# The second frame block turned once and copied out, its steps placed between the passes of the first products

## The chip, the cores and the metric

The kernel runs on one core of one Trainium2 chip. The core has five engines that run side by side: TensorE (PE, matrix products and transposes), VectorE (DVE), ScalarE (ACT), GpSimd (POOL) and SyncE (SP, which here only issues transfers). The metric is the device time of one execution in microseconds (us), as the median of the runs shown. Times of single steps come from the trace of one profiled execution.

## The reference, cut to what matters

One layer of a trunk works on 2048 prompt frames and 32 sample frames (2080 rows, 1024 wide). What concerns the change is the normalisation of the frames and the first projection:

```python
def rmsnorm(x, g):
    y = x32 * lax.rsqrt(jnp.mean(x32 * x32, axis=-1, keepdims=True) + EPS)
    return (y * g.astype(jnp.float32)).astype(x.dtype)

def layer(h, p, ...):
    hn = rmsnorm(h, g_mix)
    proj = hn @ w_in
    hA, bA, cA, zA, vB, zB = jnp.split(proj, ...)
    yA, new_conv = short_conv_mixer(hA, bA, cA, zA, ...)
    yB, new_pool = pooling_mixer(vB, zB, ...)
    h = h + jnp.concatenate([yA, yB], axis=-1) @ w_out
    gate = jax.nn.sigmoid(rmsnorm(h, g_ple) @ w_ple_gate)
    h = h + (p @ w_ple) * gate
    return h, new_conv, new_pool
```

`w_in` has 6 times 512 columns (h, b, c, za, v, zb). A final normalisation closes the trunk.

## The kernel before, in words

**Split numbers.** Products run on values split in two parts, a rounded high part and the remainder (hi and lo). One product is three matmuls: hi times hi, hi times lo, lo times hi. ScalarE makes the hi part by a copy with a cast (line 77), VectorE the lo part by a subtraction (line 78); `put` and `split` do both.

**Blocks, groups, units.** The 2080 frames are five blocks of 416 (`NB`); groups 0 and 1 have two blocks each, group 2 the last. The projection is done in units: one group and one of four 128-wide column slices `j`. Unit 0 is plain (`Unit.plain`): for each of six weights (zb, v, c, then h, za, b) and each of the two blocks, eight chunks of the 1024 rows times three split terms are 24 matmuls of 128x416 (line 571; the very first one, zb of block 0, by line 586 in the order of its split terms). Units 1 to 7 use seven half products in place of eight (`Unit.seven`, `pair`) on sums of the frames (`B["T1"]` to `B["T4"]`) and sums of the weights (`pair_weights`). Units 1 to 3 store two of these weight sums in memory (`kept_...`, lines 552 and 553), and units 4 to 7 load them again.

**Frames.** A block is three tiles of 128 frames and a short one of 32; the short tile of block 1 shares its load with that of block 0 (`short0`). A tile is loaded (line 392), its sum of squares is taken on ScalarE (line 88), the reciprocal root on GpSimd (lines 69 and 73), VectorE scales it by this and the gain row `g_bc` (`normal`, line 406), TensorE turns it in two halves of four 128x128 transposes into a bank of PSUM (`turn`, line 413), and the bank is split into the frames' pieces `B`. The gain row itself is spread over the partitions by two matmuls (`gm`, line 375) and copied by VectorE (line 376).

**Second block.** `second_block` is a generator. Its steps are: three loads with sums and normals; four turnings of which the pieces "12" and "22" are split (`pt1`); and four steps that turn the tile once more (`pt2`) and make from the two banks and the first block's pieces the sums T1 to T4 (line 619, with a ScalarE copy of one bank in line 626). `Unit.plain` calls a step between its products by hand: two behind zb, two behind v and three behind c of block 0, then one each at later places.

**Later columns.** While units 1 to 3 run, `next_columns` prepares the second group's frames column by column (the short column first, then 0, 1, 2): loads, sums, normals, turnings (`pt_g`, kept in program order), and seven pieces that are staged in tiles and stored by GpSimd's queue (line 482). The staged tiles and the frame tiles share one ring of five places (`xin`). The frames of the following column are loaded at step 5 of a column.

**Order.** Each engine runs its instructions in one order; a scheduler fills it in from dependences, and `keep_in_program_order` (or the flag `later`) holds single instructions at the place where the code has them. Transfers are issued in order by the queue of an engine: SP's for loads and stores of results, GpSimd's for the staged and the kept stores. PSUM has eight banks: six of the ring `bank` and two of the ring `tbank`.

Of the kernel before, what the change touches and what calls it, by code (L numbers as in the profile page):

```python
# [9 lines left out]
F32 = mybir.dt.float32  # L10
# [24 lines left out]
def trunk(ctx, tc, x_p, x_s, c_conv, c_pool, p_p, p_s, g_mix, w_in, conv_w, conv_b, pool_w,  # L35
# [19 lines left out]
    def tbank(name):  # L55
        return ps_t.tile([P, 512], F32, tag="tr", name=name)
# [273 lines left out]
    with ExitStack() as s1:  # L330
# [38 lines left out]
        nc.sync.dma_start(gm_row, g_mix)  # L369
        ones = ftile("ones").rearrange("p k n -> p (k n)")[:1, :P]  # L370
        nc.vector.memset(ones, 1.0)
        for half in range(2):
            cs = slice(half * NH, half * NH + NH)
            pg = tbank(f"gm_{half}")
            nc.tensor.matmul(pg, ones, gm_row[:, cs], start=True, stop=True)
            nc.vector.tensor_copy(g_bc[:, cs], pg)


        hn = {}
# [21 lines left out]
        def x_tile(name, rows):  # L401
            return x_stat(x_load(name, rows))
# [123 lines left out]
        def pair_weights(gi, ka, kb, j, name, ring, s_ring):  # L526

            s_t = (wk.tile([P, KH, P], F32, tag="s", bufs=1, name=f"s_{name}") if s_ring is None else
                   s_ring(f"s_{name}"))
            ra = raw_weight(ka, j, f"{name}a", ring)
            a11, a12 = ra[:, :KH], ra[:, KH:]
            sub = lambda o, x, y: nc.vector.tensor_tensor(o, x, y, op=ALU.subtract)
            if (ka, j) in kept:
                k1, k3 = kept.pop((ka, j))
                rb = ring(f"raw_{name}b")
                col = cols[kb] * WA + j * P
                nc.sync.dma_start(s_t, k1)  # L540
                nc.sync.dma_start(rb[:, :KH], k3)
                nc.sync.dma_start(rb[:, KH:], w_in[NH:, col:col + P].rearrange("(k p) n -> p k n", p=P))
                s3, a22 = rb[:, :KH], rb[:, KH:]
            else:
                rb = raw_weight(kb, j, f"{name}b", ring)
                a21, a22 = rb[:, :KH], rb[:, KH:]
                nc.vector.tensor_tensor(s_t, a21, a22, op=ALU.add)
                sub(a21, a11, a21)
                s3 = a21
                if gi == 0:  # L550
                    kept[ka, j] = k1, k3 = [tc.dram_tile([P, KH, P], F32, name=f"kept_{name}_{q}") for q in (1, 3)]
                    nc.gpsimd.dma_start(k1, s_t)
                    nc.gpsimd.dma_start(k3, s3)
            src = {"11": a11, "12": a12, "S2": a11, "S1": s_t, "S3": s3, "S4": a12, "22": a22}

            def make(q):
                if q == "S2":
                    sub(a11, s_t, a11)
                if q == "S4":
# [11 lines left out]
                    nc.tensor.matmul(ps[:, :NB], lhs[:, k, x], b[:, k, y], start=start and k + q == 0,  # L571
                                     stop=stop and k == KH - 1 and q == 2, skip_group_check=True)

        begun = []

        def project(ps, w, tb):
            x = hn[tb]
            if begun:
                for half in range(2):
                    half_product(ps, w[half], x[half], half == 0, half == 1)  # L580
                return

            begun.append(tb)
            steps = sorted(((k, a, b) for k in range(KC) for a, b in ((0, 0), (0, 1), (1, 0))), key=lambda t: t[1:])
            for i, (k, a, b) in enumerate(steps):
                nc.tensor.matmul(ps[:, :NB], w[k // KH][:, k % KH, a], x[k // KH][:, k % KH, b], start=i == 0,
                                 stop=i == len(steps) - 1)


        B0 = {}  # L590
        ahead0 = [x_tile(f"0_{c}", [x_rows(0, c)]) for c in range(3)]
        short0 = x_tile("0_3", [x_rows(0, 3), x_rows(1, 3)])
        B0.update(six(0))
        for c, x in enumerate([*ahead0, short0]):
            normal(x)
            n = P if c < 3 else DEC
            for half, q in enumerate(("11", "21")):
                put(B0[q][:, :, :, c * P:c * P + n], turn(x, half, f"pt0_{c}_{half}", bank)[:, :, :n])
        hn[0] = B0["11"], B0["21"]
        first_w.extend([weights(kind, 0, f"first{kind}") for kind in ("zb", "v", "c")])  # L600
        B0["12"] = piece_of(seventh("B0_12"), 0)
        hn[1] = B0["12"], B0["22"]

        def second_block():

            spans = [(c, slice(c * P, min(NB, c * P + P))) for c in range(4)]
            xs = []
            for c in range(3):
                x = x_tile(f"1_{c}", [x_rows(1, c)])
                normal(x)  # L610
                xs.append((x, slice(0, P)))
                yield
            xs.append((short0, slice(DEC, 2 * DEC)))
            for c, cs in spans:
                x = xs[c][0]
                for half, q in enumerate(("12", "22")):
                    put(B0[q][:, :, :, cs], turn(x, half, f"pt1_{c}_{half}", bank)[:, :, xs[c][1]])
                yield
            op = lambda o, a, b, op=ALU.subtract: nc.vector.tensor_tensor(o, a, b, op=op)
            for c, cs in spans:  # L620
                x, ts = xs[c]
                n = ts.stop - ts.start
                t1, t3, t2, t4 = (ftile(f"f{t}_1_{c}")[:, :, :n] for t in range(4))
                part = lambda q, h: B0[q][:, :, h, cs].bitcast(F32)
                p12 = turn(x, 0, f"pt2_{c}_0")[:, :, ts]
                nc.scalar.copy(t3, p12)
# [42 lines left out]
        class Unit:  # L669
# [98 lines left out]
            def plain(self):  # L768
                tbs, j, tag, zs, V, U, c_s = self.tbs, self.j, self.tag, self.zs, self.V, self.U, self.c_s
                blocks = range(len(tbs))  # L770

                def product_of(kind, b, w):
                    ps = bank(f"{kind}{tag}_{tbs[b]}")
                    project(ps, w, tbs[b])
                    return ps[:, :NB]
# [14 lines left out]
                if len(tbs) > 1:  # L790

                    wc = weights("c", j, f"c{tag}")
                    for b in blocks:
                        zb_block(b)
                        if b == 0:
                            for _ in range(2):
                                next(second)
                        v_block(b)
                        if b:
                            self.mix(b - 1)  # L800
                            next(second)
                        else:
                            for _ in range(2):
                                next(second)
                        c_block(b)
                        if b == 0:
                            for _ in range(3):
                                next(second)
# [697 lines left out]
```

## Time and profile before

| what | us |
|---|---|
| median of 3 runs (lowest to highest) | 945.69 (944.71 to 946.76) |
| the profiled execution | 946.5 |
| its span, first to last instruction | 944.7 |
| TensorE busy | 922.9 |
| VectorE, ScalarE, GpSimd busy | 717.3, 481.3, 137.0 |
| unit 0, from its first product to unit 1's first | 16.44 to 80.86 |
| group 0 (units 0 to 3) and unit 4's start | 16.44 to about 250 |

A row of the timeline gives a start, a length, the engine and the line of the kernel, the operation, output and inputs, the shape, the number of instructions that follow each other, and in brackets how long the engine stood idle in front and what released it. Matmuls overlap, so the time per instruction is read from starts, not from single lengths. PE is TensorE's matmul side, SPq and POOLq are the queues that issue transfers.

### The profile page before, as it was taken

How to read it: one execution, taken by the hardware profiler on the slowest of the kernel's cores; microseconds unless marked ns; L12 is line 12 of the kernel's file. 1: busy time of each engine (PE TensorE's matmuls, PEld its weight loads, DVE VectorE, ACT ScalarE, POOL GpSimd, SP SyncE). 2: the span in 40 equal slices, each digit the busy share in tenths (PEclk: the TensorE clock that was granted, in tenths of full speed). 3: DMA queues.
4: the chain of work that ended last, by engine and by line, in shares of the span. 5: the costliest groups of instructions: out<-in, count | busy, mean ns of one | idle time of the engine just before them, and what ended most of it. 6: DMA issues, size and time to landing. Idle time of an engine off the chain costs nothing.

```text
span 944.7 us, 13128 instructions
## 1 busy us (share of the span) xinstructions
PE 922.9 (98%) x4599; PEld 832.6 (88%) x4599; DVE 717.3 (76%) x1212; ACT 481.3 (51%) x890; POOL 137.0 (14%) x262
## 2 busy tenths in 40 slices
PE   7999999898999999999999999999999999999996
PEld 5999999898999999999999987888878868888885
DVE  6797998788676877776777588766554798888995
ACT  5554555463344554443554356434434885556564
POOL 2202333230100120000000011211111000211113
PEclk9999999999999999999999999999999999999999
DMA  8347686686972554618655349875785884566562
GB/s 252 95 125 199 190 262 215 198 247 182 417 253 90 180 185 131 208 57 291 177 175 174 129 145 315 270 199 159 222 255 160 309 277 127 198 232 222 207 206 111
DMA packets 132639, 190.05 MB, mean 201 GB/s; under 512 B 11740, under 2 KB 101084, under 8 KB 131293
## 3 DMA queue, kind: packets, MB, share of 16 engines
q1 hardware_dynamic: 115149, 134.06, 45.4%
q0 software_dynamic: 14688, 49.65, 16.0%
q10 hardware_dynamic: 2736, 5.51, 1.8%
q8 instruction: 36, 0.59, 0.3%
q14 instruction: 30, 0.25, 0.1%
HBM read 129.59 MB, written 59.58 MB: 200 GB/s over the span
## 4 chain that ended last, share of the span: by engine, by line
PE 77%; DVE 2%; ACT 1%; issue 0%; POOL 0%; POOLq 0%; ACTq 0%
PE x_o L167 9%; PE x_g L167 9%; PE x_zab L571 5%; PE e L102 5%; PE z_g L167 5%; PE x_ch L571 5%; PE x_zbv L571 5%; PE z_o L167 4%; PE z_ch L571 3%; PE z_zbv L571 2%; PE z_zab L571 2%; PE y_g L167 2%; PE y_o L167 2%; PE b L571 2%; PE za L571 2%; PE c L571 2%
## 5 line engine op out<-in xcount | busy, mean ns | idle before, releaser
L77 ACT CAST y_S<-y_fS 128x512 fp32r<-128x512 f32 x32 | 19.5, 621 | 43.9 <-PE x_o L167 19.4
L102 PE MATMUL e<-wq,pps 128*128 128x512 f32 (+1 forms) x156 | 38.9, 399 | 0.2 <-ACT pps L77 0.2
L571 PE MATMUL z_ch<-B,w_ch_S 128*128 128x416 f32 x168 | 35.9, 364 | 3.3 <-ACT U L866 3.3
L406 DVE SCALAR_TENSOR_TENSOR xt<-xt,rstd_x,g_bc 128x1024 f32<-128x1024 f32 (+2 forms) x18 | 23.1, 1282 | 19.1 <-POOL rstd_x L73 17.7
L571 PE MATMUL x_zab<-B,w_zab_S 128*128 128x416 f32 x168 | 34.6, 353 | 2.7 <-ACT V L866 2.0
L571 PEld LDWEIGHTS z_ch<-B,w_ch_S 128*128 128x128 f32 x168 | 32.4, 195 | 4.1 <-ACT U L866 3.6
L167 PE MATMUL x_g<-wg_b,g_S 128*128 128x512 f32 x128 | 35.9, 390 | 0.0
L167 PE MATMUL x_o<-wo_b,y_S 128*128 128x512 f32 x128 | 35.8, 391 | 0.0
L571 PEld LDWEIGHTS x_zab<-B,w_zab_S 128*128 128x128 f32 x168 | 31.1, 188 | 4.0 <-ACT V L866 2.6
L571 PE MATMUL z_zab<-B,w_zab_S 128*128 128x416 f32 x168 | 34.1, 351 | 0.5 <-ACT U L866 0.5
L571 PE MATMUL z_zbv<-B,w_zbv_S 128*128 128x416 f32 x168 | 34.2, 352 | 0.0
L571 PE MATMUL x_zbv<-B,w_zbv_S 128*128 128x416 f32 x168 | 34.1, 351 | 0.0
L571 PE MATMUL x_ch<-B,w_ch_S 128*128 128x416 f32 x168 | 34.0, 351 | 0.0
L102 PEld LDWEIGHTS e<-wq,pps 128*128 128x128 f32 (+1 forms) x156 | 27.4, 182 | 6.9 <-ACT pps L77 0.5
L571 PEld LDWEIGHTS z_zab<-B,w_zab_S 128*128 128x128 f32 x168 | 31.3, 188 | 1.1 <-ACT U L866 0.8
L69 POOL TENSOR_SCALAR ms_f<-ssq_f 128x1 f32<-128x1 f32 (+1 forms) x15 | 8.8, 588 | 160.7 <-ACT junk L88 160.7
L571 PEld LDWEIGHTS x_ch<-B,w_ch_S 128*128 128x128 f32 x168 | 31.4, 188 | 0.3
L571 PEld LDWEIGHTS x_zbv<-B,w_zbv_S 128*128 128x128 f32 x168 | 31.3, 188 | 0.3
L571 PEld LDWEIGHTS z_zbv<-B,w_zbv_S 128*128 128x128 f32 x168 | 31.2, 188 | 0.4
L77 ACT CAST y<-y 128x512 fp32r<-128x512 f32 x24 | 14.8, 618 | 28.7 <-PE x_o L167 14.0
L1328 DVE SCALAR_TENSOR_TENSOR h<-h,rstd_f,g_bc 128x1024 f32<-128x1024 f32 (+1 forms) x15 | 19.3, 1284 | 12.7 <-POOL rstd_f L73 12.7
L167 PEld LDWEIGHTS x_o<-wo_b,y_S 128*128 128x128 f32 x128 | 24.0, 188 | 5.1 <-ACT c_o L1132 0.3
(582 smaller groups left out, 2670.8 us busy)
## 6 DMA issues: line engine op xcount, KB each, us to landing
y<-y_d SPq DMA_DIRECT2D x16, 512.0 KB, 7.7
x<-in_x_prompt_dram SPq DMA_DIRECT2D x16, 512.0 KB, 6.7
h_d<-x SPq DMA_DIRECT2D x16, 512.0 KB, 3.4
h<-h_d SPq DMA_DIRECT2D x16, 512.0 KB, 5.1
xt<-in_x_prompt_dram SPq DMA_DIRECT2D x15, 512.0 KB, 12.0
e<-e_d SPq DMA_DIRECT2D x15, 512.0 KB, 5.1
out_dram<-h POOLq DMA_DIRECT2D x14, 512.0 KB, 3.0
p_dT<-T POOLq DMA_DIRECT2D x12, 512.0 KB, 5.3
```

The source lines that it names most:

```text
L69: nc.gpsimd.tensor_scalar(ms[:n], ssq[:n], scalar1=1.0 / D, scalar2=EPS, op0=ALU.mult, op1=ALU.add)
L77: ins = nc.scalar.copy(hi, src)
L102: nc.tensor.matmul(ps[:n], pps[:, a, k, :n], wp[k][b][:, cs], start=k + q == 0, stop=k == 1 and q == 2)
L167: nc.tensor.matmul(ps[:n], lhs[:, k, a, :n], w[b][:, k], start=start and k + q == 0, stop=k == KH - 1 and q == 2, skip_group_check=True)
L406: nc.vector.scalar_tensor_tensor(xt[:n], xt[:n], r[:n], g_bc[:n], op0=ALU.mult, op1=ALU.mult)
L571: nc.tensor.matmul(ps[:, :NB], lhs[:, k, x], b[:, k, y], start=start and k + q == 0, stop=stop and k == KH - 1 and q == 2, skip_group_chec ...
L1328: nc.vector.scalar_tensor_tensor(h[:n], h[:n], rf[:n], g_bc[:n], op0=ALU.mult, op1=ALU.mult)
```

## The change: what it does

- **Beginning.** The two `gm` matmuls stay in their banks `pg`; block 0's normals multiply from there, in halves of 512 (`first_normal`), and ScalarE copies the gain row out later. Seven, two, three and two transposes of the identity into the short tile's bank are put between the turnings of block 0 (`fill`). The hi and lo parts of block 0 and of the first weights are written out in an order by hand (`first_hi`, `first_lo`), one hi part on VectorE.
- **First products.** zb, v and c of block 0 are computed together (`first_products`), each in a bank of its own, in three passes: hi times hi for all three, then weight hi times frame lo, then weight lo times frame hi. Two steps of the second block (loads and normals of its first two tiles) stand before the second pass, the third tile's before the third pass, and one turning stands before each of the three products of the third pass and one behind them. All are held in program order. The lo parts of v's and c's weights are made in the third pass.
- **Second block.** Each of its tiles is turned once. The bank is split into the pieces and also copied by ScalarE into the tile's own place (`turned`); the sums read that copy. The 32 transposes and four copies of the second turning are gone, eight copies are new.
- **Transfers.** The kept stores go from GpSimd's queue to SP's. The next column's frames are loaded at step 7 of a column, not 5.

```diff
+        pg = [tbank(f"gm_{half}") for half in range(2)]
         for half in range(2):
-            cs = slice(half * NH, half * NH + NH)
-            pg = tbank(f"gm_{half}")
-            nc.tensor.matmul(pg, ones, gm_row[:, cs], start=True, stop=True)
-            nc.vector.tensor_copy(g_bc[:, cs], pg)
+            nc.tensor.matmul(pg[half], ones, gm_row[:, half * NH:half * NH + NH], start=True, stop=True)
+
+        def fill(n, t):
+
+            for _ in range(n):
+                tc.keep_in_program_order(nc.tensor.transpose(t[:, :P], ident, ident))
+
+        short_bank = bank("pt0_3")
+        fill(7, short_bank)
...
-                    nc.gpsimd.dma_start(k1, s_t)
-                    nc.gpsimd.dma_start(k3, s3)
+                    nc.sync.dma_start(k1, s_t)
+                    nc.sync.dma_start(k3, s3)
...
+        def first_products(ws):
+            x = hn[0]
+            out = {kind: bank(f"{kind}0_0_0") for kind in ws}
+            for a, b in ((0, 0), (0, 1), (1, 0)):
+                if b:
+                    next(second)
+                    next(second)
+                for kind, w in ws.items():
+                    if a:
+                        if kind == "zb":
+                            next(second)
+                            first_los["v"]()
+                        elif kind == "v":
+                            first_los["c"]()
+                        next(second)
+                    for k in range(KC):
+                        ins = nc.tensor.matmul(out[kind][:, :NB], w[k // KH][:, k % KH, a], x[k // KH][:, k % KH, b],
+                                               start=a + b + k == 0, stop=a == 1 and k == KC - 1, skip_group_check=True)
+                        if a + b + k or kind != "zb":
+                            in_turn(ins)
+            next(second)
+            return out
...
+        def first_normal(x):
+            xt, m, r = x
+            for half in range(2):
+                h = xt[:m, half * NH:half * NH + NH]
+                in_turn(nc.vector.scalar_tensor_tensor(h, h, r[:m], pg[half][:m], op0=ALU.mult, op1=ALU.mult))
...
+        def first_tile(c):
+            first_normal(first_x[c])
+            turned_x[c] = first_turn(c, first_x[c])
+            if c < 3:
+                fill((2, 3, 2)[c], short_bank)
...
+        for half in range(2):
+            nc.scalar.copy(g_bc[:, half * NH:half * NH + NH], pg[half])
...
             for c, cs in spans:
-                x = xs[c][0]
+                x, ts = xs[c]
+
+                turned = x[0].rearrange("p (k t) -> p k t", k=KC)[:, :, :ts.stop - ts.start]
                 for half, q in enumerate(("12", "22")):
-                    put(B0[q][:, :, :, cs], turn(x, half, f"pt1_{c}_{half}", bank)[:, :, xs[c][1]])
+                    pt = turn(x, half, f"pt1_{c}_{half}", bank)[:, :, ts]
+                    put(B0[q][:, :, :, cs], pt)
+                    nc.scalar.copy(turned[:, half * KH:half * KH + KH], pt)
+                whole.append((turned[:, :KH], turned[:, KH:]))
                 yield
...
-                p12 = turn(x, 0, f"pt2_{c}_0")[:, :, ts]
-                nc.scalar.copy(t3, p12)
                 op(t1, p12, part("11", 0))
-                p22 = turn(x, 1, f"pt2_{c}_1")[:, :, ts]
-                op(t3, p22, t3)
+                op(t3, p22, p12)
...
                     wc = weights("c", j, f"c{tag}")
+                    first.update(first_products(dict(zb=wz, v=wv, c=wc)))
                     for b in blocks:
                         zb_block(b)
-                        if b == 0:
-                            for _ in range(2):
-                                next(second)
                         v_block(b)
...
-                    if i == 5 and after is not None:
+                    if i == 7 and after is not None:
                         load_ahead(1, after)
```

More of the change, by code (lines that the diff above doesn't have):

```diff
@@ L572, in half_product @@
                                      stop=stop and k == KH - 1 and q == 2, skip_group_check=True)
-        begun = []
         def project(ps, w, tb):
             x = hn[tb]
[L578 to L587, printed above, removed]
+            for half in range(2):
+                half_product(ps, w[half], x[half], half == 0, half == 1)
@@ L590, in trunk @@
         B0 = {}
-        ahead0 = [x_tile(f"0_{c}", [x_rows(0, c)]) for c in range(3)]
-        short0 = x_tile("0_3", [x_rows(0, 3), x_rows(1, 3)])
+        ahead0 = [x_load(f"0_{c}", [x_rows(0, c)]) for c in range(3)]
+        short0 = x_load("0_3", [x_rows(0, 3), x_rows(1, 3)])
         B0.update(six(0))
-        for c, x in enumerate([*ahead0, short0]):
-            normal(x)
-            n = P if c < 3 else DEC
-            for half, q in enumerate(("11", "21")):
-                put(B0[q][:, :, :, c * P:c * P + n], turn(x, half, f"pt0_{c}_{half}", bank)[:, :, :n])
@@ L599, in trunk, with in_turn, first_turn @@
-        hn[0] = B0["11"], B0["21"]
-        first_w.extend([weights(kind, 0, f"first{kind}") for kind in ("zb", "v", "c")])
+        def in_turn(ins):
+            tc.keep_in_program_order(ins)
+        def first_normal(x):
[3 more added lines that the diff above has]
+                in_turn(nc.vector.scalar_tensor_tensor(h, h, r[:m], pg[half][:m], op0=ALU.mult, op1=ALU.mult))
+        def first_turn(c, x):
+            xt, m, _ = x
+            if c < 3:
+                return [turn(x, half, f"pt0_{c}_{half}", bank) for half in range(2)]
+            t = short_bank
+            for k in range(KC):
+                tc.keep_in_program_order(nc.tensor.transpose(t[:, k * m:k * m + m], xt[:m, k * P:(k + 1) * P], ident[:m, :m]))
+            t = t.rearrange("p (k t) -> p k t", k=KC)
+            return t[:, :KH], t[:, KH:]
@@ new lines, in trunk, with place0, first_hi, first_lo @@
+        first_x, turned_x = [], {}
+        def place0(c, half):
+            n = P if c < 3 else DEC
+            piece = B0[("11", "21")[half]][:, :, :, c * P:c * P + n]
+            return piece[:, :, 0], piece[:, :, 1], turned_x[c][half][:, :, :n]
+        def first_hi(c, half, copy=nc.scalar.copy):
+            hi, _, src = place0(c, half)
+            in_turn(copy(hi, src))
+        def first_lo(c, half):
+            hi, lo, src = place0(c, half)
+            in_turn(nc.vector.tensor_tensor(lo, src, hi.bitcast(F32), op=ALU.subtract))
@@ new lines, in first_tile @@
+        def first_tile(c):
+            first_normal(first_x[c])
+            turned_x[c] = first_turn(c, first_x[c])
+            if c < 3:
+                fill((2, 3, 2)[c], short_bank)
+        for c in range(3):
+            first_x.append(x_stat(ahead0[c], True))
+        first_tile(0)
+        first_hi(0, 0)
+        first_x.append(x_stat(short0, True))
+        short0 = first_x[3]
+        first_tile(1)
+        first_hi(0, 1)
+        first_lo(0, 0)
+        for half in range(2):
+            first_hi(1, half)
@@ new lines, in trunk @@
+        first_tile(2)
+        first_hi(2, 0)
+        first_tile(3)
+        first_hi(2, 1, nc.vector.tensor_copy)
+        raw = raw_weight("zb", 0, "firstzb")
+        first_zb = [wtile(f"w_firstzb_{half}") for half in range(2)]
+        for half, t in enumerate(first_zb):
+            in_turn(nc.scalar.copy(t[:, :, 0], raw[:, half * KH:half * KH + KH]))
+        for half in range(2):
+            first_hi(3, half)
+        for c in range(4):
+            for half in range(2):
+                if c + half:
+                    first_lo(c, half)
@@ new lines, in trunk, with other_first, los @@
+        hn[0] = B0["11"], B0["21"]
+        for half, t in enumerate(first_zb):
+            nc.vector.tensor_tensor(t[:, :, 1], raw[:, half * KH:half * KH + KH], t[:, :, 0].bitcast(F32), op=ALU.subtract)
+        first_w.append(first_zb)
+        first_los = {}
+        def other_first(kind):
+            raw = raw_weight(kind, 0, f"first{kind}")
+            ts = [wtile(f"w_first{kind}_{half}") for half in range(2)]
+            for half, t in enumerate(ts):
+                nc.scalar.copy(t[:, :, 0], raw[:, half * KH:half * KH + KH])
+            def los():
+                for half, t in enumerate(ts):
+                    nc.vector.tensor_tensor(t[:, :, 1], raw[:, half * KH:half * KH + KH], t[:, :, 0].bitcast(F32),
+                                            op=ALU.subtract)
+            first_los[kind] = los
+            return ts
@@ L601, in trunk @@
+        first_w.extend(other_first(kind) for kind in ("v", "c"))
+        for half in range(2):
+            nc.scalar.copy(g_bc[:, half * NH:half * NH + NH], pg[half])
         B0["12"] = piece_of(seventh("B0_12"), 0)
@@ L613, in second_block @@
             xs.append((short0, slice(DEC, 2 * DEC)))
+            whole = []
             for c, cs in spans:
-                x = xs[c][0]
+                x, ts = xs[c]
+                turned = x[0].rearrange("p (k t) -> p k t", k=KC)[:, :, :ts.stop - ts.start]
                 for half, q in enumerate(("12", "22")):
-                    put(B0[q][:, :, :, cs], turn(x, half, f"pt1_{c}_{half}", bank)[:, :, xs[c][1]])
+                    pt = turn(x, half, f"pt1_{c}_{half}", bank)[:, :, ts]
+                    put(B0[q][:, :, :, cs], pt)
+                    nc.scalar.copy(turned[:, half * KH:half * KH + KH], pt)
+                whole.append((turned[:, :KH], turned[:, KH:]))
                 yield
@@ L620, in second_block @@
             for c, cs in spans:
-                x, ts = xs[c]
-                n = ts.stop - ts.start
+                p12, p22 = whole[c]
+                n = cs.stop - cs.start
                 t1, t3, t2, t4 = (ftile(f"f{t}_1_{c}")[:, :, :n] for t in range(4))
                 part = lambda q, h: B0[q][:, :, h, cs].bitcast(F32)
-                p12 = turn(x, 0, f"pt2_{c}_0")[:, :, ts]
-                nc.scalar.copy(t3, p12)
                 op(t1, p12, part("11", 0))
-                p22 = turn(x, 1, f"pt2_{c}_1")[:, :, ts]
-                op(t3, p22, t3)
+                op(t3, p22, p12)
                 op(t1, t1, part("11", 1))
@@ L770, in plain @@
                 blocks = range(len(tbs))
+                first = {}
                 def product_of(kind, b, w):
+                    if b == 0 and kind in first:
+                        return first.pop(kind)[:, :NB]
                     ps = bank(f"{kind}{tag}_{tbs[b]}")
@@ L801, in plain @@
                             next(second)
-                        else:
-                            for _ in range(2):
-                                next(second)
                         c_block(b)
-                        if b == 0:
-                            for _ in range(3):
-                                next(second)
                     self.mix(1)
```

## The prediction

> **What bounds the kernel now.** I read the page first (busy times, then the chain that ended last).
>
> ```profile
> span 944.7 us, 13128 instructions
> PE 922.9 (98%) x4599; PEld 832.6 (88%) x4599; DVE 717.3 (76%) x1212; ACT 481.3 (51%) x890; POOL 137.0 (14%) x262
> PE 77%; DVE 2%; ACT 1%; issue 0%; POOL 0%; POOLq 0%; ACTq 0%
> ```
>
> TensorE is busy for 922.9 of 944.7 us: only work taken off it, a faster clock, or less idle time counts. The view of busy time by stretches, cut at the edges of the first unit, tells where its 21.8 us of idle time are (columns: length, then PE busy and so on, granted clock, DMA share, GB/s).
>
> ```profile
> 0.00:16.40 16.40, 10.62 (x36) 6.78 (x36) 9.12 (x13) 9.84 (x18) 5.90 (x45) 1.00 0.87 226
> 16.40:80.68 64.28, 64.28 (x361) 62.42 (x360) 55.12 (x105) 32.99 (x65) 9.49 (x14) 1.00 0.47 135
> 80.68:250.00 169.32, 161.95 (x864) 157.10 (x863) 144.74 (x248) 86.98 (x166) 42.99 (x63) 0.99 0.74 235
> ```
>
> Idle are 5.8 us at the start, 7.4 us in units 1 to 4, the rest behind. The first unit, which the change rewrites, has none: there only fewer or faster TensorE instructions help. The timeline of TensorE shows both.
>
> ```profile
> 2.27 3.74 PE L375 MATMUL gm<-gm_row,ones 1*128 1x512 f32 x4 [2.27 <-DVE V L699]
> 8.30 3.98 PE L413 MATMUL pt<-ident,xt 128*128 128x128 f32 x16 [2.28 <-DVE xt L406]
> 12.99 1.97 PE L413 MATMUL pt<-ident,xt 128*128 128x128 f32 x8 [0.72 <-DVE xt L406]
> 15.42 1.09 PE L413 MATMUL pt<-ident,xt 64*128 64x64 f32 x8 [0.46 <-PE pt L413]
> 16.44 3.14 PE L586 MATMUL zb<-B,w_firstzb 128*128 128x416 f32 x8
> 19.72 2.40 PE L586 MATMUL zb<-B,w_firstzb 128*128 128x416 f32 x11
> 23.01 2.23 PE L571 MATMUL v<-B,w_firstv 128*128 128x416 f32 x11
> 32.77 2.55 PE L413 MATMUL pt<-ident,xt 128*128 128x128 f32 x24
> 36.35 0.60 PE L413 MATMUL pt<-ident,xt 128*128 128x128 f32 x4
> 71.69 9.33 PE L571 MATMUL b<-B,w_b 128*128 128x416 f32 x48
> 80.86 1.49 PE L571 MATMUL x_zbv<-B,w_zbv 128*128 128x416 f32 x7
> ```
>
> From 71.69 to 80.86 48 products stand 0.191 us apart. The first 8 take 3.14 us, 0.39 each: half speed, though the clock column says 1.00 there. The transposes show it too: 0.249 each at 8.30, 0.103 each at 32.77 (24 up to 35.25).
>
> **The second turning goes: -3.2 us.** Before, the second block's frames are turned twice, 32 transposes each time (36.35 x4 is the first of the second turning); after, the bank is copied out and the sums read the copy. From 23.01 to 80.86, 57.85 us, stand 263 products of 416 columns and 6 of the mixing: 269 x 0.191 = 51.4. The other 6.5 us are 64 transposes, so 32 cost 3.2 (24 in 2.48 gives 3.3). It is time of the engine that has no gap there, so it is on the path.
>
> **The clock in the first products: -1.7 us.** Between 16.44 and 23.01 lie 25 products and one transpose; at full speed 25 x 0.191 + 0.13 = 4.9, they take 6.57. After, 14 transposes of the identity (7, 2, 3 and 2) fill TensorE's gaps from about 6.0, where the row at 2.27 ends, to the first product; I take the whole difference, as if the clock were up by then. Bounds 0 and 1.7; which holds depends on whether transposes count as activity, taken up among the rivals.
>
> **The beginning: -0.6 us.** The two copies of the gain row leave DVE, and the normals read the bank in halves.
>
> ```profile
> 6.06 0.69 DVE L376 COPY g_bc<-gm 128x512 f32<-128x512 f32 x1 [1.02 <-PE gm L375]
> 6.96 1.28 DVE L406 SCALAR_TENSOR_TENSOR xt<-xt,rstd_x,g_bc 128x1024 f32<-128x1024 f32 x1 [0.21 <-ACT junk L88]
> 12.85 1.28 DVE L78 TENSOR_TENSOR B<-pt,B 128x512 fp32r<-128x512 f32 x2
> 14.05 1.27 DVE L406 SCALAR_TENSOR_TENSOR xt<-xt,rstd_x,g_bc 64x1024 f32<-64x1024 f32 x1
> 16.12 0.27 ACT L77 CAST B<-pt 128x128 fp32r<-128x128 f32 x1
> ```
>
> The third frame tile is bound by its load, but one of the two remainders in front of the short tile (12.85) moves behind it, so the short normal starts at about 13.3 instead of 14.05 and its last cast, behind the two weight casts of 0.52 each, ends about 16.05. The first product needs only the first of the two casts: 15.85 instead of 16.44. If TensorE is still at half speed, 24 transposes x 0.249 + 8 x 0.136 + 14 x 0.249 from 6.0 end at 16.6, and nothing is gained. Bounds -0.7 and +0.2.
>
> **A new wait behind the third pass: +1.0 us.** In the passes all three first products share three of the six banks. The four frame turnings stand between the products of the third pass, and ScalarE must cast and now also copy each bank before it is used again.
>
> ```profile
> L77 ACT CAST B<-pt 128x512 fp32r<-128x512 f32 (+1 forms) x9 | 3.7, 498 | 0.2 <-PE pt L413 0.2
> L626 ACT COPY f<-pt 128x512 f32<-128x512 f32 (+1 forms) x4 | 2.0, 507 | 2.2 <-PE pt L413 2.2
> 10.61 1.05 ACT L77 CAST B<-pt 128x512 fp32r<-128x512 f32 x2
> ```
>
> TensorE: from 15.85, 48 products of passes 1 and 2 (9.2) and the transpose of 0.13 lead to 25.2; the first half of a turning is ready at 25.6; 24 products (4.6) and 32 transposes (3.3) end at 33.1. ScalarE has from 25.6 on 6 casts and 6 copies of 512, 4 small ones and 3 evacuations. By duration (0.53, 0.27 and 0.51 each; the last two as in the copies' row) that is 9.0 us and ends at 34.6; back to back two casts of 0.59 take only 1.05, 0.47 apart, and with 0.47, 0.2 and 0.45 it is 7.8 and ends at 33.4. The second block's first product needs the last cast: 1.5 or 0.3 us. I take 1.0, nearer the long one, since most casts start singly, after a half turning. Outer bounds: 0, and 3.2 where all six copies (0.53) come to stand in front of TensorE. From 34.1, 222 products and mixings (42.4) lead to 76.5, against 80.86.
>
> DVE has 55.12 of 64.28 us busy in this unit and loses none of its sums, but gets them in the first product's time instead of 45 to 80: its remainders for the next weights come earlier. Worth nothing while TensorE has no gap. The eight half normals replace four (8 x 0.65 against 4 x 1.28): nothing.
>
> **The moved transfers: 0.** The kept stores (256 KB) go from POOL's queue to SP's and stand there ahead of weight loads; until now such a load waited for the same DVE result by way of its tile. One load is held much longer, the second raw tile of unit 1's c/h pair; it now waits for the zb/v pair's sums.
>
> ```profile
> 45.73 0.68 DVE L535 TENSOR_TENSOR raw_zbv_1b<-raw_zbv_1a,raw_zbv_1b 128x512 f32<-128x512 f32 x1
> 78.30 0.68 DVE L547 TENSOR_TENSOR s_ch<-raw_ch_1b 128x512 f32<-128x512 f32 x1
> 125.48 0.82 SPq L392 DMA_DIRECT2D xt<-in_x_prompt_dram  x2
> 128.13 0.85 POOL L482 DMA_DIRECT2D p_d<-21_1_0_1368  x1 [3.64 <-DVE 21_1_0_1368 L78]
> p_d<-21_1_0_1368 POOLq DMA_DIRECT2D x1, 512.0 KB, 4.9
> xt<-in_x_prompt_dram SPq DMA_DIRECT2D x6, 512.0 KB, 6.2
> xt<-in_x_prompt_dram SPq DMA_DIRECT2D x15, 512.0 KB, 12.0
> 133.66 0.38 SPq L508 DMA_DIRECT2D raw_zab_2a<-in_w_in_dram  x1
> 142.25 1.06 ACT L88 ACTIVATE junk<-xt 128x1024 bf16<-128x1024 f32 x1
> 146.36 1.28 DVE L406 SCALAR_TENSOR_TENSOR xt<-xt,rstd_x,g_bc 128x1024 f32<-128x1024 f32 x1 [0.22 <-POOL rstd_x L73]
> 148.58 1.04 PE L413 MATMUL pt_g<-ident,xt 128*128 128x128 f32 x8
> ```
>
> In DVE's new order the sum of 45.73 stands behind the second block's sums, by my count of its instructions near 67; the tile's own sum (78.30) is due at about 74. Some 7 us are enough for its load; were they not, DVE would hold back remainders of unit 1's products.
>
> The frame loads of the following column are issued two steps later, and take the places of two staged stores: SP waits until the store of 128.13 has landed (133.0, in the new times 4.5 earlier, 128.5), where it waited for a turning until 125.48. Behind them in SP's queue stands the weight load of 133.66 (new 129.2): not held. With 6.2 us they land at 134.7, and their sum of squares (142.25) is due at 137.75: 3.0 us to spare.
>
> **Sum:** -3.2 - 1.7 - 0.6 + 1.0 = **-4.5 us**. The profiled execution took 946.5 us (its span of 944.7 and 1.8 around it), 0.8 above the median of 945.69, inside the runs' 944.71 to 946.76. 946.5 - 4.5 = 942.0, so for the median **941.2**. From unit 1 on everything shifts as it is, the idle 7.4 us included.
>
> **The rivals.**
>
> *The clock stays down.* For: 16 transposes filled 8.30 to 12.30 (3.98 of 4.00) and the short tile's still took 0.136 each; full speed came only some 3.5 us into the products (the 11 from 19.72 stand 0.21 apart). Against: no stretch before that was without a gap for more than 4 us, and after there is one of some 4 us of transposes behind 3.7 of gain products. Then -3.2 + 0.1 + 1.0 = -2.1: 943.6. The Trainium skill ("TensorE: Matmul & The Clock Gate", Part 4: PE-mode transpose) says that the full clock does not engage for transposes, as they don't count as busy in the same way; by it, this rival is the outcome. Its Part 1 says that one free-running window of 3.4 us of sustained activity releases the clock; the trace agrees as far as products go (16.44 to about 20), and no run here shows yet what transposes alone do.
>
> *Frames too late, slower.* Place: the pair of frame loads above. For: all frame loads have a median of 12.0, which is 2.8 late. Against: those of this stretch, 6.2. When the pair lands after 137.75, ScalarE stands in its order with the next weights' casts behind, then POOL, two DVE normals, and the turning of 148.58, which starts 0.94 after the last normal. Each us above 0.9 is TensorE's, and a wait of about 3 us also costs clock, as one in unit 3 does now:
>
> ```profile
> 215.24 2.43 PE L571 MATMUL x_ch<-B,w_ch_S 128*128 128x416 f32 x12
> 220.92 4.09 PE L571 MATMUL z_ch<-B,w_ch_S 128*128 128x416 f32 x12 [3.26 <-ACT U L866]
> 221.00:225.00 4.00, 4.00 (x13) 3.82 (x14) 3.59 (x6) 1.66 (x3) 0.00 (x0) 0.57 0.04 15
> ```
>
> Twelve products take 4.09 instead of 2.43 there, +1.7. Landing 6 us late costs 5.1 + 1.7 - 4.5 = +2.3: 948.0. It decides for slower from 3.7 us late (2.8 + 1.7 against 4.5), a landing of 12.9 us.
>
> *The gain is waited away later.* The wait of 3.26 goes back to loads:
>
> ```profile
> DVE s_zab L547 <- DMA raw_zab_3b<-in_w_in_dram: 4.6, 1, 4.6
> ```
>
> If such loads land at fixed times (the DMA share is 0.74 in those units), TensorE arrives 4.5 earlier and waits 4.5 longer: 945.7, no change. Against: their issue hangs on buffers that TensorE and DVE release, which shifts along.
>
> *That stall goes.* The kept stores and frame loads that share the DMA engines with those loads come at other times. Without its 3.26 and 1.7: 941.2 - 5.0 = 936.2.
>
> **How the numbers follow.** Forecast 0.42 (941.2; its own range 939.8 to 943.4, from a third-pass wait of 0 to 3.2 and the beginning's bounds), clock down 0.24 (943.6), late frames 0.19 (945 to 950), waited away 0.08, stall gone 0.07. The range leaves out the end of the last and the worst late frames: 938.0 to 947.8. What a measurement can tell from no change is 0.2%, 1.9 us: 943.8 to 947.6. Faster: 0.42 + 0.07 + half of the clock's 0.24 + 0.02 of the waiting = 0.63. Same: 0.12 + 0.06 + 0.03 of late frames = 0.21. Slower: 0.16.
>
> **What would show it.** The first unit's last product ends near 76.5 instead of 80.86, with 32 transposes fewer. The first products stand 0.19 apart from about 15.9 (right), or 0.38 until about 20 (clock down). A gap of 0.3 to 1.5 us, waiting for ScalarE, stands before the second block's first product. The sums of squares of the second column start near 138 with no wait for their loads, and the turning near 144.1 follows without a gap. The stall of 3.3 us comes back near 213. The forecast is wrong if TensorE's idle time from 76.5 to 245.5 differs from 7.4 by more than 2 us.

## The result, and the profile after

The changed kernel takes 936.37 us (median of 5 runs, 935.15 to 938.27), the kernel before 946.11 (5 runs, 944.71 to 946.84): 0.9901 of it, 95% interval 0.9889 to 0.9914, some 9.4 us less. The profiled execution is the fastest of the five, 935.15. The page has these rows for it (span, busy times, the chain that ended last):

```profile
span 933.4 us, 13100 instructions
PE 917.5 (98%) x4581; PEld 827.8 (89%) x4581; DVE 716.9 (77%) x1215; ACT 482.2 (52%) x895; POOL 126.3 (14%) x244
PE 75%; DMA 2%; ACT 2%; issue 1%; DVE 1%; POOL 0%; POOLq 0%; DVEq 0%; ACTq 0%
```

TensorE is busy 5.4 us less and idle 5.9 us less. The busy time by stretches, cut at the changed kernel's own edges (first product, first product of unit 1):

```profile
0.00:14.56 14.56, 11.28 (x50) 8.10 (x51) 7.87 (x15) 10.13 (x20) 4.83 (x45) 1.00 0.91 246
14.56:74.54 59.98, 59.59 (x328) 58.03 (x328) 56.11 (x106) 34.14 (x69) 7.79 (x10) 1.00 0.52 151
74.54:250.00 175.46, 171.91 (x921) 166.22 (x921) 149.19 (x254) 91.25 (x175) 34.48 (x49) 1.00 0.79 252
```

Unit 0 starts 1.9 us earlier and is 4.4 us shorter (64.42 before). In units 1 to 3 behind it TensorE is idle for 3.5 us instead of 7.4. TensorE's timeline of the beginning, and its waits over the whole execution:

```profile
6.12 1.76 PE L379 MATMUL pt<-ident 128*128 128x128 f32 x7
9.37 0.63 PE L379 MATMUL pt<-ident 128*128 128x128 f32 x2
9.80 1.51 PE L419 MATMUL pt<-ident,xt 128*128 128x128 f32 x8
11.14 0.49 PE L379 MATMUL pt<-ident 128*128 128x128 f32 x3
11.46 1.19 PE L419 MATMUL pt<-ident,xt 128*128 128x128 f32 x8
14.56 1.75 PE L605 MATMUL zb<-B,w_firstzb 128*128 128x416 f32 x8 [0.83 <-DVE B L651]
19.29 1.68 PE L605 MATMUL zb<-B,w_firstzb 128*128 128x416 f32 x8
26.99 0.66 PE L419 MATMUL pt<-ident,xt 128*128 128x128 f32 x4 [0.17 <-ACT zs L893]
32.40 0.46 PE L577 MATMUL zb<-B,w_firstzb 128*128 128x416 f32 x1 [0.22 <-ACT B L77]
...
PE z_ch L577 <- ACT U L973: 0.9, 1, 0.9
PE x_zab L577 <- ACT V L973: 0.3, 1, 0.3
```

The first eight products take 1.75 us where they took 3.14, about 0.2 apart from the first one on, and before that the transposes go from 0.215 (two from 9.37 to 9.80) to 0.107 (three from 11.14 to 11.46). The waits for U and V were 3.3 and 2.0 us before.

Which part does what is read from two lengths, both differences of starts in TensorE's timeline: unit 0 from its first product to unit 1's first (x_zbv), and units 1 to 3 with the start of unit 4 (x_zbv to x_zbv). From there to the end every profile below takes 700.2 to 702.5. The two profiles of the changed kernel differ by 2.2 us in units 1 to 3, so differences between single profiles are good to about that.

| kernel | first product | unit 0 | units 1 to 3 |
|---|---|---|---|
| before | 16.44 | 64.42 | 163.26 |
| changed, two profiles | 14.56, 14.57 | 59.98, 59.98 | 158.55, 160.73 |

### The profile page after: what moved, and what is told of

It is laid out like the page before. It is cut to its first block, busy times and chain, and to the rows that moved or that the text cites. A ratio compares the mean times of both kernels' runs of the same rounds, so it can differ in the third digit from the quotient of the medians.

```text
span 933.4 us, 13100 instructions
## 1 busy us (share of the span) xinstructions
PE 917.5 (98%) x4581; PEld 827.8 (89%) x4581; DVE 716.9 (77%) x1215; ACT 482.2 (52%) x895; POOL 126.3 (14%) x244
## 4 chain that ended last, share of the span: by engine, by line
PE 75%; DMA 2%; ACT 2%; issue 1%; DVE 1%; POOL 0%; POOLq 0%; DVEq 0%; ACTq 0%
PE x_o L167 9%; PE x_g L167 9%; PE x_zab L577 5%; PE e L102 5%; PE z_g L167 5%; PE z_o L167 4%; PE x_ch L577 4%; PE x_zbv L577 4%; PE z_zab L577 2%; PE y_g L167 2%; PE z_ch L577 2%; PE y_o L167 2%; PE b L577 2%; PE z_zbv L577 2%; PE c L577 2%; PE v L577 2%
## 5 line engine op out<-in xcount | busy, mean ns | idle before, releaser
L69 POOL TENSOR_SCALAR ms_f<-ssq_f 128x1 f32<-128x1 f32 (+1 forms) x15 | 8.8, 588 | 160.7 <-ACT junk L88 160.7
L77 ACT CAST y<-y 128x512 fp32r<-128x512 f32 x24 | 14.9, 620 | 28.7 <-PE z_o L167 12.8
L412 DVE SCALAR_TENSOR_TENSOR xt<-xt,rstd_x,g_bc 128x1024 f32<-128x1024 f32 (+2 forms) x14 | 17.9, 1282 | 13.9 <-POOL rstd_x L73 12.7
```

Source lines behind the costliest of these rows:

```text
L69: nc.gpsimd.tensor_scalar(ms[:n], ssq[:n], scalar1=1.0 / D, scalar2=EPS, op0=ALU.mult, op1=ALU.add)
L77: ins = nc.scalar.copy(hi, src)
L412: nc.vector.scalar_tensor_tensor(xt[:n], xt[:n], r[:n], g_bc[:n], op0=ALU.mult, op1=ALU.mult)
```

## The experiments

**The two transfer edits, undone one at a time.**

```diff
-                    nc.sync.dma_start(k1, s_t)
-                    nc.sync.dma_start(k3, s3)
+                    nc.gpsimd.dma_start(k1, s_t)
+                    nc.gpsimd.dma_start(k3, s3)
```

> The changed kernel with one edit undone: the kept stores go back to GpSimd's queue. Theory Q (the kept stores on SP's queue, waiting there for VectorE, hold back unit 4's weight loads, so that unit 3's last weight tile lands earlier): SP issues the load of raw_ch_0a about 1 us behind raw_zab_3b again (after: 9 us), VectorE waits for raw_zab_3b some 4 us, TensorE waits about 3 us for U near 210 and runs a stretch at half clock: 940.5 to 941.5 us. Theory S (the frame loads two steps later did it) and theory C (it is only that everything comes earlier): no such wait, within 1 us of 936.4.

Measured: 939.11 us, 0.9935 of before (0.9914 to 0.9956). The wait is back, the stretch at half clock isn't, and the time lies below the 940.5 to 941.5 that were expected with it. VectorE's, SP's and TensorE's timelines of this run:

```profile
193.37 0.59 SPq L514 DMA_DIRECT2D raw_zab_3b<-in_w_in_dram  x1
194.52 7.17 SPq L514 DMA_DIRECT2D raw_ch_0a<-in_w_in_dram  x1
208.28 0.69 DVE L553 TENSOR_TENSOR s_zab<-raw_zab_3b 128x512 f32<-128x512 f32 x1 [3.91 <-DMA raw_zab_3b<-in_w_in_dram]
214.42 2.53 PE L577 MATMUL z_ch<-B,w_ch_S 128*128 128x416 f32 x12 [2.62 <-ACT U L973]
```

The load is used 14.9 us after its issue (208.28 - 193.37). In the changed kernel it is 13.1, and there VectorE waits last for a store to leave a tile:

```profile
191.97 0.69 SPq L514 DMA_DIRECT2D raw_zab_3b<-in_w_in_dram  x1
193.82 6.54 SPq L558 DMA_DIRECT2D kept_ch<-s_ch  x1
201.13 0.45 SPq L514 DMA_DIRECT2D raw_ch_0a<-in_w_in_dram  x1
205.06 0.69 DVE L553 TENSOR_TENSOR s_zab<-raw_zab_3b 128x512 f32<-128x512 f32 x1 [2.15 <-DMA kept_ch<-s_ch]
211.20 2.53 PE L577 MATMUL z_ch<-B,w_ch_S 128*128 128x416 f32 x12 [0.88 <-ACT U L973]
```

The second edit:

```diff
-                    if i == 7 and after is not None:
+                    if i == 5 and after is not None:
```

> The changed kernel with one edit undone: the next column's frames are loaded at step 5 again. Theory S: the wait of about 3 us near 210 comes back, 940.5 to 941.5 us. Theories Q and C: the wait stays under 1 us, within 1 us of 936.4. In either case SP issues the second column's frame loads near 119 instead of 122.6, as they wait for turnings again and not for staged stores.

Measured: 939.07 us, 0.9931 (0.9911 to 0.995). Neither theory's place: the wait for U stays at 0.8, but the one for V, 45 us earlier, is back, and this time with half clock behind it (two rows of TensorE's timeline, one of the stretches):

```profile
168.52 0.72 PE L577 MATMUL x_zab<-B,w_zab_S 128*128 128x416 f32 x2 [2.48 <-ACT V L973]
169.85 3.83 PE L577 MATMUL x_zab<-B,w_zab_S 128*128 128x416 f32 x10 [0.61 <-DVE w_zab_S L78]
170.00:175.00 5.00, 5.00 (x15) 4.77 (x16) 5.00 (x9) 2.42 (x4) 0.00 (x0) 0.50 0.36 124
```

So there are two waits; the kept stores act on the one for U, the step on what stands in front of the one for V. What the later step does is seen on ScalarE. Before, two casts into staged places wait there one after the other, each for a store; the casts of the next weights stand behind them:

```profile
168.42 0.62 ACT L77 CAST T<-f_g 128x512 fp32r<-128x512 f32 x1 [7.19 <-DMA p_d<-21_1_1_1710]
169.95 0.62 ACT L77 CAST T<-f_g 128x512 fp32r<-128x512 f32 x1 [0.90 <-DMA p_d<-22_1_1_1730]
170.90 0.62 ACT L77 CAST w_zab_S<-raw_zab_2a 128x512 fp32r<-128x512 f32 x1 [0.33 <-DVE raw_zab_2a L535]
```

After, only the last piece waits, and the weights follow 0.53 later; the copy of V, for which TensorE waits, stands behind three such casts of the weights. The other waits for stores are now those of the frame loads, on SP:

```profile
154.97 0.63 ACT L77 CAST T<-f_g 128x512 fp32r<-128x512 f32 x1
162.53 0.62 ACT L77 CAST T<-f_g 128x512 fp32r<-128x512 f32 x1 [6.93 <-DMA p_d<-22_1_1_1711]
163.06 0.62 ACT L77 CAST w_zab_S<-raw_zab_2a 128x512 fp32r<-128x512 f32 x1
```

In every profile of this document two casts wait so with step 5, and one with step 7.

**Both undone, and both alone on the kernel before.**

> The changed kernel with both transfer edits undone (kept stores on GpSimd's queue, frame loads at step 5). Each undone alone cost about 3 us. If they act on different waits (the kept stores on the wait for U near 211, the frame loads on others), both cost 5 to 7 us: 941.5 to 943. If they act on the same crowd of transfers, it is 3 to 4: 939 to 940.5.

> The kernel before with only the two transfer edits. Theory Q+S (the transfers by themselves take out the wait of 3.3 us near 218 and its stretch at half clock): 3 to 6 us faster than before, the first unit unchanged with its first x_zbv product near 80.9. Theory C (they pay only where the first unit ends earlier), and the prediction's price of nothing for them: within 1 us of before.

> The kernel before with only the kept stores on SP's queue. Theory Q: raw_ch_0a is issued some 8 us behind raw_zab_3b, and TensorE's wait for U near 218 falls from 3.3 to under 1.5 us: 2 to 5 us faster than before. If the kept stores only pay together with the later frame loads: within 1 us of before.

> The kernel before with only the frame loads moved to step 7. If the wait for staged places leaves ScalarE's queue for SP's (only the last staged piece of a column waits for a store): ScalarE is free about 1 to 2 us earlier near 170, TensorE's wait for V near 174 falls from 2 to 3 us to under 1.5, the wait for U near 218 stays at about 3: 1 to 3 us faster than before. If the frame loads only pay together with the kept stores: within 1 us of before.

> The changed kernel itself once more, for its spread and a second profile beside the next three on one chip: 936 to 938 us. If the short wait near 211 (0.9 us) of the first profile was the edits' doing, this profile shows under 1.5 us there again; if it was luck of that run, it shows 2.5 us or more.

| kernel | us, ratio to before (interval) | units 1 to 3 | wait for V, for U |
|---|---|---|---|
| changed, again | 937.39, 0.9897 (0.988 to 0.9915) | 160.73 | 1.6, 1.0 |
| changed, both undone | 942.70, 0.9954 (0.9936 to 0.9972) | 162.84 | 0.8, 3.1 |
| before, with both | 942.93, 0.9956 (0.994 to 0.9973) | 159.90 | 1.4, 1.4 |
| before, kept stores only | 944.35, 0.9974 (0.9957 to 0.9991) | 162.98 | 3.2, 1.0 |
| before, step 7 only | 944.88, 0.9994 (0.9976 to 1.0011) | 161.10 | 0.2, 2.9 |

The transfers alone are worth 0.0044 of 947.5 us, 4.2 us, and the rest of the change without them 0.0046, 4.4 us; together that is 8.6 of the 9.4 to 9.8 measured. Each of the two is known to about 1.7 us, and within that they add up. Sorted by the two edits, units 1 to 3 last 163.3 and 162.8 with neither, 161.8 and 161.1 with the step alone, 163.0 and 160.9 with the kept stores alone, and 158.6, 159.9 and 160.7 with both; three more kernels with both, further down, have 159.2, 159.4 and 161.3 (the last waits 2.1 us at another place). Two rows need the clock beside the wait for V: 1.6 us in the first is followed by a stretch at a granted clock of 0.71, and 0.8 us in the second by one at 0.66, both from 170 to 175.

The wait for U follows the kept stores without exception: 2.6 to 3.3 us in the four profiles with all of them on GpSimd's queue, 0.8 to 1.6 in the nine with SP's (one of these, further down, leaves out a pair). The wait for V follows the step less strictly: 0.8 to 3.2 us with step 5, at most 1.6 with step 7. The price of each edit by itself is less sure than that of both. Compared by the ratios, with and without the other edit and in the old and the new kernel, the kept stores bring 2.2 to 3.6 us and the step 0.6 to 2.8; for the step the two intervals overlap each time. The step alone on the kernel before removes its wait (0.2 us), but no gain in time is shown for it: its interval holds 1, and its profile also had a first unit 0.9 us longer than that of before (first products 22.93 instead of 21.98 at the same place). The kept stores alone took 2.3 us off the wait for U, but the wait for V grew by 1.2, with half clock behind it (a granted clock of 0.50 from 175 to 180); the 2.1 us by which that profile is shorter than that of before come from a first unit that ended 2.4 us earlier, for another reason (below, at the transposes).

**Why the kept stores matter.** One pair of them, that of unit 3's c/h weights, is left out; unit 7 adds those weights again.

```diff
-                if gi == 0:
+                if gi == 0 and (ka, j) != ("c", 3):
                     kept[ka, j] = k1, k3 = ...
```

> The changed kernel with the kept stores on GpSimd's queue and one pair of them, that of unit 3's c/h weights (0.5 MB), left out; unit 7 makes those sums again from the weights. raw_ch_0a is then issued right behind raw_zab_3b. Theory H (unit 4's loads, held back behind the kept stores on SP, made room): wait for U near 211 again 2.5 us or more, like the kept stores on GpSimd's queue, 938.5 to 940 us. Theory B (the kept pair on GpSimd's queue took the DMA engines' time beside raw_zab_3b): raw_zab_3b is there within 13.3 us of its issue instead of 14.9, the wait for U is under 1.5: 936 to 937.5.

> The changed kernel with that one pair of kept stores left out, the others on SP's queue. Theory H: unit 4's loads come right behind raw_zab_3b again, the wait for U goes to 2.5 us or more: 938 to 940 us. Theory B: no store stands beside or behind the load, VectorE need not wait for the store of s_ch to leave its tile, the wait for U is 1 us or less: 935.5 to 937.5, a candidate to beat the change.

Measured: 938.31 us (0.9917, 0.9892 to 0.9942) with the others on GpSimd's queue, 935.91 (0.9899, 0.9878 to 0.9919) with them on SP's. The first of the two, in SP's, VectorE's and TensorE's timelines:

```profile
194.94 0.63 SPq L514 DMA_DIRECT2D raw_zab_3b<-in_w_in_dram  x1
196.12 6.97 SPq L514 DMA_DIRECT2D raw_ch_0a<-in_w_in_dram  x1
207.52 0.69 DVE L553 TENSOR_TENSOR s_zab<-raw_zab_3b 128x512 f32<-128x512 f32 x1 [1.81 <-DMA raw_zab_3b<-in_w_in_dram]
213.66 2.53 PE L577 MATMUL z_ch<-B,w_ch_S 128*128 128x416 f32 x12 [0.53 <-ACT U L973]
```

raw_ch_0a follows 1.2 us behind raw_zab_3b, as before, and still the load is used 12.6 us after its issue, not 14.9, and TensorE waits 0.5 us. Holding unit 4's loads back is not what helps (theory H falls); the half megabyte on GpSimd's queue beside the load is what cost 2.3 us (theory B). All profiles agree: from issue to use the load takes 14.6 to 14.9 us in the four with all kept stores on GpSimd's queue, and 12.8 to 13.3 in the eight with them on SP's, where VectorE's last wait is for a store and not for the load. The DMA engines are full all that time (busy share 1.05 over the 14.9 us, 1.06 over the 12.6, at 302 and 293 GB/s); half a megabyte at that rate is 1.7 us, an estimate, and so most of the 2.3. The time of this kernel alone would not have decided: 938.31 lies above theory B's 936 to 937.5, just under H's 938.5; in its profile the first product came at 16.20, 1.6 us late. The other kernel shows the same 12.6 with raw_ch_0a 1.2 behind. Its time cannot be told from the changed kernel's (0.9899 against 0.9901 and 0.9897), so no version here is shown to beat it.

**The transposes of the identity.** They are taken out, in two runs.

```diff
-        fill(7, short_bank)
...
-            if c < 3:
-                fill((2, 3, 2)[c], short_bank)
```

> The changed kernel without the 14 transposes of the identity; TensorE idles between the turnings of the first block. If they brought the clock up (theory F): turnings again 0.25 us apart, first products 0.38 apart for about 3.5 us, first product near 15.5 instead of 14.56, so 2.0 to 3.0 us slower: 938.4 to 939.4. If the gain row's matmuls and the turnings do it by themselves, or the order on VectorE sets the first product: products 0.19 apart from the start, within 0.5 us of 936.4.

> The changed kernel without the 14 transposes once more, for a second profile beside other runs. If they are what brings the clock up: again 0.38 us for the first 8 products each and the first x_zbv product 3 to 3.5 us later than 74.5, 938 to 940 us; if the first profile was an unlucky phase of the clock: products 0.19 apart within the first 8, x_zbv near 76, 937 us.

Measured: 937.26 us (0.9922, 0.9896 to 0.9948) and 940.12 (0.9938, 0.9919 to 0.9957), 2 to 4 us above the changed kernel; the interval of the first still holds the changed kernel's 0.9901, that of the second doesn't. The first median lies below what was expected, its profiled execution (941.62) above. Both profiles show the same; TensorE's timeline of the first:

```profile
7.86 3.67 PE L418 MATMUL pt<-ident,xt 128*128 128x128 f32 x16 [1.78 <-DVE xt L624]
12.35 1.97 PE L418 MATMUL pt<-ident,xt 128*128 128x128 f32 x8 [0.82 <-DVE xt L624]
15.79 3.11 PE L604 MATMUL zb<-B,w_firstzb 128*128 128x416 f32 x8 [0.43 <-ACT B L646]
22.67 1.68 PE L604 MATMUL zb<-B,w_firstzb 128*128 128x416 f32 x8
```

With gaps between the turnings the transposes stay at 0.23 to 0.24, the first products at 0.36, and unit 0 lasts 62.2 (62.6 in the second) instead of 60.0, from a start at 15.79 (16.38). In all eight profiles with the identity's transposes the first eight products take 1.73 to 1.75 us.

The old beginning does not always stay at half clock either. Of its four profiles, the one with the kept stores alone (first two rows) and the one with the step alone (last two) show this:

```profile
14.79 0.68 PE L413 MATMUL pt<-ident,xt 64*128 64x64 f32 x8 [0.46 <-PE pt L413]
15.69 1.79 PE L586 MATMUL zb<-B,w_firstzb 128*128 128x416 f32 x8 [0.22 <-ACT B L77]
13.03 1.09 PE L413 MATMUL pt<-ident,xt 128*128 128x128 f32 x8 [0.90 <-DVE xt L406]
16.47 3.14 PE L586 MATMUL zb<-B,w_firstzb 128*128 128x416 f32 x8
```

In the first, the 24 turnings of three tiles came without a gap from 8.35 on, those of the short tile then took 0.68 us instead of 1.09, and the first products ran at full speed: unit 0 lasted 62.77 instead of 64.42. In the second the third tile's turnings (1.09 instead of 1.97) already ran at full speed, and the first products behind them at half again. So transposes alone bring the clock up, with the identity's in all eight profiles in time for the first products, with the old beginning in one of four.

**The second turning put back.** The copies out of the banks go, the 32 transposes and the copy of before return.

```diff
-                    nc.scalar.copy(turned[:, half * KH:half * KH + KH], pt)
...
+                p12 = turn(x, 0, f"pt2_{c}_0")[:, :, ts]
...
+                p22 = turn(x, 1, f"pt2_{c}_1")[:, :, ts]
```

> The changed kernel with the second turning put back: the eight copies out of the banks go, 32 transposes and four copies of a turned bank come back, at the steps' new places. If the transposes cost their own length where TensorE has no gap: +3.2 us, less up to 0.4 us of wait for ScalarE in the third pass: 939.2 to 939.6. If the later waits swallow it (the wait near 211 takes up what comes earlier): within 1 us of 936.4.

Measured: 939.61 us (0.9939, 0.9921 to 0.9957), 3.6 us above the changed kernel by the ratios. Unit 0 lasts from 14.90 to 78.23, 63.33 instead of 59.98: 3.35 us.

## Why the prediction was wrong, step by step

The step that failed is "The moved transfers: 0". They brought 4.2 us, the rest of the change 4.4, where the sum said 4.5, and so the time left the range at its fast end. The prediction's own sign of being wrong came: TensorE's idle time in units 1 to 3 is 3.5 us, not 7.4. That the rest came so near to the sum is in part luck, as its terms were off in both directions (below), and the profile of the kernel without the transfers happened to start late, at 15.99. In both profiles of the changed kernel unit 1 starts 6.3 us earlier than before, not 4.4 (76.5 was forecast).

- *The transfers.* The kept stores were priced by the queue they join, where nothing waits for them. The queue they leave was not looked at: there they ran beside the late load that the same prediction names as the root of the 3.26 us wait. The frame loads were priced as a risk of landing late. They did land in time: SP issued the first at 122.58 and the second at 127.47, behind a wait of 4.4 us for a store, much as the prediction had it (128.5), and ScalarE's sums began at 136.09 and 137.66, with no wait noted in front. That their new places free ScalarE's queue of a wait for a store was in the built order and not read from it. The rival "that stall goes" had the time nearly right (936.2) and 0.07, but only a vague ground, "come at other times"; the experiments give two grounds, and only one of them is at that stall. Its 5.0 us are that stall alone, where the 4.2 measured are spread over two waits, so its nearness is in part luck too.
- *The second turning, -3.2.* Right: 3.35.
- *The clock, -1.7, and the beginning, -0.6.* The clock came up, and earlier than the sum had it: at about 11 us, so the turnings of the last tiles went at full speed too. Without the fills unit 0 is 2.2 and 2.6 us longer, somewhat more than 1.7. The first product came at 14.56, not 15.85, which is what the kernel without the fills gives (15.79). That term was mis-sized: 1.9 instead of 0.6 in this profile. It is not always that much: of eight profiles with the fills five start at 14.55 to 14.90, the others at 15.21, 15.99 and 16.20, the last of these after a wait of 2.2 us for the third tile's normal. The rival "the clock stays down" is out. By the Trainium skill ("TensorE: Matmul & The Clock Gate", Part 4: PE-mode transpose) it should have held. Here nothing but transposes ran from 6.12 to 13.7, and full speed came in the middle of them, so the measurement decides against the page.
- *The wait behind the third pass, +1.0.* It is 0.17 + 0.22 = 0.4 us, near the lower working (0.3): ScalarE's casts and copies stand mostly 0.48 apart there, nearly back to back.
- *Late frames, slower.* Not seen. *Waited away later:* not seen; units 1 to 3 last 162.84 with the new first unit and the old transfers, 163.26 before.
- *The forecast's own range.* Its bounds (a wait of 0 to 3.2, a beginning of -0.7 to +0.2) add up to 940.1 to 944.2, not 939.8 to 943.4. Nothing rests on it.

## What to carry to other kernels

When a transfer moves, price both queues: what will wait behind it where it goes, and what it shared the DMA engines with where it was; a load that is already known to be late is the first to look at. Where tiles of two kinds share a ring, a shift in the order of requests also shifts which queue waits for a store; here it went from ScalarE's to SP's, but by itself that gave no gain that could be told from none. And an idle stretch in front of the first product can be filled with transposes to raise the clock. They should leave no gap until it is up; behind that, one of 2.2 us did not bring it down again in one profile.

## What the runs showed of the hardware

- The length of a wait does not tell whether the clock drops behind it. After 2.62 us 12 products took 2.53 us, full speed; after 2.48 us the ten above took 3.83; after 2.91 and 3.26, 4.10 and 4.09. It can drop behind a short one, too: with both transfers undone ten products took 3.44 us behind 0.84 and another 0.69, against 2.17 in the changed kernel behind 0.27 and 0.69. The Trainium skill ("TensorE: Matmul & The Clock Gate", Part 1: The HAM clock gate) has a free-running window for this, which would make it a matter of phase; the runs agree with that but don't measure a window.
- The issue on SP's queue that came third behind raw_zab_3a and raw_zab_3b took 6.4 to 7.5 us in every profile, whether it was a load (7.17, 6.97) or a store (6.54), where raw_zab_3b itself took 0.6 to 0.8. Why it is held was not tried.
